# First mixer of a hybrid decoder: low parts of the weights made by accumulating loads, state scaling on VectorE

## The chip, the cores and the metric

The kernel runs on one core of a Trainium2 chip. A core has a matrix engine (TensorE, PE in the profile, with its weight loads as PEld), three engines for elementwise work (VectorE is DVE, ScalarE is ACT, GpSimd is POOL), and SyncE (SP), which here only issues transfers. The engines run their own instruction streams in order and wait for one another by semaphores. The metric is the device time of one execution in microseconds (us).

## The reference

One inference step of a small decoder: a Mamba-2 (SSD) mixer, a squared-ReLU MLP, an HGRN2 mixer and a second MLP, on 512 prompt tokens and 32 sample tokens (8 sequences of 4). Width is 1024. The change touches the SSD mixer alone; its core is

```python
proj = u @ w_in                                    # z, x/B/C, dt
xbc = silu(conv(xbc_ext) + conv_b)
def step(h, inp):                                  # chunks of 64 tokens
    ...
    y = einsum('bijgr,bjgrp->bigrp', cb * decay * dtq, xq)
    y = y + einsum('bign,bgrpn->bigrp', cq, h) * exp(cum)
    h = exp(cum[:, -1]) * h + einsum('bjgr,bjgrp,bjgn->bgrpn', tail, xq, bq)
    ...
y = group_rmsnorm((y + xs * d_skip) * silu(z), norm_w, 4)
return y @ w_out, new_conv, h
```

The line with `exp(cum[:, -1]) * h` is the state scaling that the change moves. The state is an output as well, for the prompt and for each sample sequence.

## The kernel before

All activations stay on chip, transposed: 1024 features as 8 tiles of 128 rows by 544 tokens (512 + 32). The products keep float32 accuracy by splitting both operands into a high part, which TensorE takes exactly, and the low rest, and by adding three products: high by high, high by low, low by high.

The weights of the whole network are streamed from memory as 224 units `W[u]` of 128x1024 float32 (512 KB): units 0 to 55 are the first mixer's (in and out projections interleaved), 56 to 119 the first MLP's (a Strassen form that also uses sums of blocks), 120 to 159 the second mixer's, 160 to 223 the second MLP's. A unit goes through these steps:

- `load_next` takes a buffer `raw` of the pool `wraw` (3 buffers) and issues the load on SyncE's queue (L170). In the MLPs it also forms sums `v` of two blocks, the second added by a load that accumulates, issued by GpSimd (L180).
- `conv_unit` calls `split` (L186 to L188): ScalarE casts `raw` to the high part `whi` (pool `wcv`, 2 buffers), then `wlo = raw - whi` is formed on VectorE. For units 4 to 55 whose number is divisible by 3 (17 of them) the subtraction is on GpSimd.
- `products` (L278 to L288) runs 48 matmuls for the unit.

`take` and `unit` keep the conversion one unit ahead of the products. A scheduler fixes the order of the instructions on each engine when the kernel is built, by program order and priority; `conv_unit` has high priority. Pools limit how far a step can run ahead: a tile can be written again only when the last reader of its buffer is done. PSUM has two accumulators of two banks (`acc`) and four of one bank (`mx`).

Beside the products of units 0 to 55 runs the rest of the mixer, as generators that are stepped while the products are issued: the convolution (L438 to L462: `pre`, `cacc`, `th`, `xs`), the step sizes (`dt_steps`, L771 on: `pcum`, `pdec`), and for each of 4 groups of heads `scan(g)` (L527) and `gated_norm` (L727). `scan` works on four chunks of 128 prompt tokens: `weights(c)` loads rows of the running sum (`w<-cum_d`) and takes the exponential on ScalarE, `tokens(c)` makes `xd` and `xt`, `inside(c)` computes the chunk's state contribution `pu` from `bt` and `xt`, scales the state `hT` in place (L569, GpSimd, chunks 1 to 3, so 12 times in all), adds `pu` (L570, VectorE) and adds the chunk's own output `py` to `y`; `before(c)` adds the earlier state's. Then the sample tokens: `xq` is split in two VectorE instructions (L685), the four state tiles `st` (two sequences each, 128x1024) are used in `psi`, scaled in place (L699, GpSimd, 16 in all), and 8 matmuls `pn` (L708) of `bm` and `xq` are added to them (L709, VectorE) before they are written out.

Of the kernel before, what the change touches and what calls it, by code (L numbers as in the profile page):

```python
# [10 lines left out]
F32R = mybir.dt.float32r  # L11
I32 = mybir.dt.int32
AF = mybir.ActivationFunctionType
ALU = mybir.AluOpType
ADD, SUB, MUL, MAX, MIN = ALU.add, ALU.subtract, ALU.mult, ALU.max, ALU.min

P = 128
# [31 lines left out]
U_MLP = U_SSD_OUT + 16  # L49
# [47 lines left out]
def trunk(ctx: ExitStack, tc: tile.TileContext, io):  # L97
    nc = tc.nc
# [1 line left out]

    const = ctx.enter_context(tc.tile_pool(name="const", bufs=1))
    pers = ctx.enter_context(tc.tile_pool(name="pers", bufs=1))
    wraw = ctx.enter_context(tc.tile_pool(name="wraw", bufs=3))
    wcv = ctx.enter_context(tc.tile_pool(name="wcv", bufs=2))
    psb = ctx.enter_context(tc.tile_pool(name="psb", bufs=2, space=PS))
    psm = ctx.enter_context(tc.tile_pool(name="psm", bufs=4, space=PS))
# [30 lines left out]
    loaded = {("u", i): t for i, t in enumerate(first)}  # L137
# [27 lines left out]
    def load_next():  # L165
        kind, u = loads[state["load"]]
        state["load"] += 1
        if kind == "u":
            raw = wraw.tile([P, 1024], F32, tag="raw", name=f"raw{u}")
            nc.sync.dma_start(raw, io["W"][u])  # L170
        elif kind == "a22":
            raw = mp["w"].tile([P, 512], F32, tag="a22", bufs=2, name=f"a22_{u}")
            nc.sync.dma_start(raw, io["W"][u + 1][:, 512:])
        else:

            raw = mp["w"].tile([P, 1024], F32, tag="v", bufs=3, name=f"v{u}")
            nc.sync.dma_start(raw[:, :512], io["W"][u + 1][:, 512:])
            nc.sync.dma_start(raw[:, 512:], io["W"][u][:, :512])
            for c in (0, 512):
                nc.gpsimd.dma_start(raw[:, c : c + 512], io["W"][u + 1][:, :512], accum_op=ADD)  # L180
        loaded[kind, u] = raw
# [4 lines left out]
    def split(raw, hi, lo, eng=None):  # L186
        nc.scalar.copy(hi, raw)  # L187
        (eng or nc.vector).tensor_tensor(lo, raw, hi.bitcast(F32), SUB)  # L188

    def conv_unit():  # L190
        if state["conv"] >= len(jobs):
            return
        (kind, u), at = jobs[state["conv"]]
        state["conv"] += 1
        with tc.high_priority() if u > 2 else ExitStack():
            while state["load"] <= min(at + (3 if mp else 1), len(loads) - 1):
                if loads[state["load"]][0] != "u" and not mp:
                    break
                load_next()
        with tc.high_priority() if u > 2 and not mp else ExitStack():  # L200
            if kind == "u":
                raw = loaded.pop(("u", u))
                hi = wcv.tile([P, 1024], F32R, tag="whi", name=f"whi{u}")
                lo = wcv.tile([P, 1024], F32R, tag="wlo", name=f"wlo{u}")
                for a in (0, 512) if u < 2 else (None,):
                    c = slice(None) if a is None else slice(a, a + 512)
                    split(raw[:, c], hi[:, c], lo[:, c], nc.gpsimd if 3 < u < U_MLP and u % 3 == 0 else None)
            else:
                hi, lo = form(kind, u)
        ready[kind, u] = (hi, lo)  # L210

    def form(name, u):

        a1 = loaded["u", u]
        v = loaded.get(("v", u))
        if name == "n6":
            s2 = mp["w"].tile([P, 512], F32, tag="s2", bufs=2, name=f"s2_{u}")
            nc.vector.tensor_tensor(s2, v[:, :512], a1[:, :512], ADD)
            loaded["s2", u] = s2
        if name == "q7":  # L220
            s2 = loaded["s2", u]
            nc.vector.tensor_tensor(s2, s2, a1[:, 512:], ADD)
        raw = {
            "p1": lambda: a1[:, :512], "p2": lambda: a1[:, 512:], "n6": lambda: s2, "q7": lambda: v[:, 512:],
            "n5": lambda: v[:, :512], "p3": lambda: loaded["s2", u], "q4": lambda: loaded["a22", u],
        }[name]()
        hi = mp["w"].tile([P, 512], F32R, tag="fh", bufs=5, name=f"fh{u}_{name}")
        lo = mp["w"].tile([P, 512], F32R, tag="fl", bufs=5, name=f"fl{u}_{name}")
        split(raw, hi, lo)
        return hi, lo  # L230

    def take(key):
        i = place[key]
        ahead = 0.0
        j = i
        while j + 1 < len(jobs) and ahead < 1.0:
            j += 1
            ahead += 1.0 if jobs[j][0][0] == "u" else 0.25
        while state["conv"] <= j:
            if jobs[state["conv"]][0][0] != "u" and not mp:  # L240
                break
            conv_unit()
        return ready.pop(key)
# [50 lines left out]
    def mx(name):  # L294
        return psm.tile([P, 512], F32, tag="mx", name=name)
# [82 lines left out]
    def ssd(then):  # L378
# [23 lines left out]


        conv_unit()
        conv_unit()
        xh = [pool.tile([P, 4, T], F32R, tag="y", bufs=2, name=f"xh{i}") for i in range(2)]
        xops = []
        for k in range(KT):
            lo = pool if k < 4 else p2
            lo = lo.tile([P, T], F32R, tag=f"yh{k}" if k < 4 else ("BT", "CT")[k % 2], name=f"xl{k}")  # L410
# [116 lines left out]
        def scan(g, BT, CT, xs, par):  # L527

            cum_d, dec, tok, ttok, etok = par
            pace = PACE[g]  # L530
            hs = slice(8 * g, 8 * g + 8)
# [28 lines left out]
            def inside(c):  # L560

                cs = slice(c * P, (c + 1) * P)
                pu = mx(f"pu{g}_{c}")
                nc.tensor.matmul(pu, bt[:, c], xts[c].rearrange("p h q -> p (h q)"), start=True, stop=True)
                if c == 0:
                    nc.scalar.copy(hT, pu)
                else:
                    hv = hT.rearrange("p (h q) -> p h q", q=64)
                    nc.gpsimd.tensor_tensor(hv, hv, dec[:, hs, c : c + 1].to_broadcast([P, 8, 64]), MUL)  # L569
                    nc.vector.tensor_tensor(hT, pu, hT, ADD)  # L570
                py = mx(f"py{g}_{c}")
                for h in range(8):
                    nc.tensor.matmul(
                        py[64 * (h % 2) : 64 * (h % 2) + 64, (h // 2) * P : (h // 2 + 1) * P], xds[c][:, h], ws_[c][:, h],
                        start=True, stop=True,
                    )
                nc.vector.tensor_tensor(y[:, :, cs], py.rearrange("p (j t) -> p j t", t=P), y[:, :, cs], ADD)
# [110 lines left out]
            for s in range(SEQS):  # L688
                c = s % 4
# [6 lines left out]
                ysc, psi.rearrange("p (h q) -> p h q", q=64), etok[:, hs].unsqueeze(2).to_broadcast([P, 8, 64]), MUL  # L696
            )
            for q in range(4):
                nc.gpsimd.tensor_tensor(  # L699
                    sts[q].rearrange("p s (h q) -> p s h q", q=64), sts[q].rearrange("p s (h q) -> p s h q", q=64),  # L700
                    dec[:, hs, 4 + 2 * q : 6 + 2 * q].rearrange("p h s -> p s h").unsqueeze(3).to_broadcast([P, 2, 8, 64]), MUL,
                )
# [815 lines left out]
```

## Time and profile before

| quantity | value |
|---|---|
| median of 3 runs | 1586.72 us (1585.82 to 1588.2) |
| the profiled execution | 1590.45 us |
| its span in the trace | 1588.7 us |
| mean granted TensorE clock | 0.985 |
| memory traffic | 164.00 MB read, 17.18 MB written |
| weight units on GpSimd (wlo, L188) | 17, mean 2.485 us |
| weight loads on SyncE (raw) | 198 of 512 KB, median 3.6 us to landing |

The profile gives, for one execution, the busy time of each engine, the TensorE clock that was granted, who waited for whom, and groups of like instructions. `out<-in` names the tile that an instruction writes and those it reads, with the buffer numbers left out; L188 is line 188 of the kernel. The lines themselves are shown where they are used.

### The profile page before, as it was taken

The page shows a single profiled execution, that of the slowest core. Times are in us where ns is not written, and L with a number is a line of the kernel's source. Part 1 is how long each engine was busy: PE and PEld are TensorE (multiplying, and loading weights), DVE is VectorE, ACT ScalarE, POOL GpSimd, SP SyncE. Part 2 cuts the span into 40 slices and gives each one's busy share as a digit, 9 for nine tenths or more (in the row PEclk, how much of TensorE's full clock was granted, in tenths as well). Part 3 has the DMA queues.
Part 4 walks back from the last instruction along what each step waited for, and adds up shares of the span by engine and source line. Part 5 has one row for each costly group of instructions (what it writes and reads, how often), then busy time and mean ns, then how long its engine had stood idle before and what let it go on. Part 6 is the DMA issues. An engine that isn't in the chain of part 4 may idle for free.

```text
span 1588.7 us, 32391 instructions
## 1 busy us (share of the span) xinstructions
PE 1547.5 (97%) x13420; PEld 1482.7 (93%) x13420; DVE 1099.3 (69%) x1962; ACT 741.9 (47%) x1431; POOL 187.9 (12%) x208
## 2 busy tenths in 40 slices
PE   8898989999999999999999999999999999999997
PEld 7896879999999999999999999999999999999997
DVE  7888787877887747464565688888878655474644
ACT  5585663757434526353463333333335436273552
POOL 4323141232311001010000000000001001010001
PEclk9998998999999999999999999999999999999998
DMA  5353435354236236344323232323226335453311
GB/s 185 104 164 105 159 88 187 102 176 143 74 120 175 91 107 172 94 136 104 112 64 126 67 96 83 98 83 116 77 94 173 88 106 153 120 160 80 120 54 57
DMA packets 88116, 183.28 MB, mean 115 GB/s; under 512 B 12641, under 2 KB 39297, under 8 KB 87969
## 3 DMA queue, kind: packets, MB, share of 16 engines
q1 hardware_dynamic: 79792, 167.49, 33.7%
q0 software_dynamic: 6912, 12.59, 4.9%
q8 instruction: 105, 1.72, 0.5%
q10 hardware_dynamic: 1264, 1.14, 0.2%
q14 instruction: 43, 0.34, 0.1%
HBM read 164.00 MB, written 17.18 MB: 114 GB/s over the span
## 4 chain that ended last, share of the span: by engine, by line
PE 71%; DVE 4%; ACT 1%; DMA 1%; issue 1%; POOL 0%; POOLq 0%; SPq 0%; ACTq 0%; DVEq 0%
PE pd L284 22%; PE ps L284 15%; PE pp L973 11%; PE pm L284 6%; PE pc L973 4%; PE pho L284 3%; PE po L284 2%; PE pa L1112 1%; DVE wlo L188 1%; ACT whi L187 1%; DMA raw<-in_W 1%; PE pS L1215 0%; PE po L1238 0%; PE pa L1131 0%; PE pd L1342 0%
## 5 line engine op out<-in xcount | busy, mean ns | idle before, releaser
L187 ACT CAST whi<-raw 128x1024 fp32r<-128x1024 f32 (+1 forms) x178 | 185.0, 1039 | 344.7 <-PE ps L284 110.7
L188 DVE TENSOR_TENSOR wlo<-raw,whi 128x1024 fp32r<-128x1024 f32 (+1 forms) x161 | 200.5, 1245 | 31.0 <-ACT whi L187 27.0
L284 PE MATMUL pd<-gh,wlo 128*128 128x272 f32 x992 | 205.5, 288 | 0.9 <-DVE wlo L188 0.6
L284 PE MATMUL pd<-gh,whi 128*128 128x272 f32 x992 | 205.7, 287 | 0.0
L284 PE MATMUL pd<-gl,whi 128*128 128x272 f32 x992 | 205.0, 288 | 0.0
L284 PEld LDWEIGHTS pd<-gh,wlo 128*128 128x128 f32 x992 | 155.7, 188 | 2.2 <-DVE wlo L188 2.2
L284 PEld LDWEIGHTS pd<-gh,whi 128*128 128x128 f32 x992 | 156.2, 188 | 0.0
L284 PEld LDWEIGHTS pd<-gl,whi 128*128 128x128 f32 x992 | 155.6, 188 | 0.0
L284 PE MATMUL ps<-uh_s,whi 128*128 128x272 f32 x576 | 127.4, 303 | 1.6 <-DVE zs L503 0.8
L373 DVE TENSOR_TENSOR x<-pd,x 128x544 f32<-128x544 f32 x62 | 44.7, 722 | 121.3 <-PE pd L284 121.3
L284 PE MATMUL ps<-ul_s,whi 128*128 128x272 f32 x576 | 122.5, 294 | 0.5 <-DVE ul_s L188 0.5
L284 PE MATMUL ps<-uh_s,wlo 128*128 128x272 f32 x576 | 121.7, 293 | 0.0
L180 POOL DMA_DIRECT2D v<-in_W x48 | 42.3, 1045 | 593.0 <-DMA v<-in_W 448.6
L284 PE MATMUL ps<-uh,whi 128*128 128x272 f32 x512 | 112.2, 300 | 0.0
L284 PE MATMUL ps<-uh,wlo 128*128 128x272 f32 x512 | 106.8, 288 | 0.0
L284 PE MATMUL ps<-ul,whi 128*128 128x272 f32 x512 | 106.4, 289 | 0.0
L284 PEld LDWEIGHTS ps<-uh_s,whi 128*128 128x128 f32 x576 | 93.0, 194 | 9.7 <-issue 5.6
L284 PEld LDWEIGHTS ps<-ul_s,whi 128*128 128x128 f32 x576 | 93.6, 195 | 1.0 <-DVE ul_s L188 0.7
L284 PEld LDWEIGHTS ps<-uh_s,wlo 128*128 128x128 f32 x576 | 92.7, 193 | 0.1
L284 PEld LDWEIGHTS ps<-uh,whi 128*128 128x128 f32 x512 | 80.6, 189 | 3.8 <-issue 1.4
L284 PEld LDWEIGHTS ps<-ul,whi 128*128 128x128 f32 x512 | 80.3, 189 | 0.0
L284 PEld LDWEIGHTS ps<-uh,wlo 128*128 128x128 f32 x512 | 80.2, 188 | 0.0
(428 smaller groups left out, 3894.1 us busy)
## 6 DMA issues: line engine op xcount, KB each, us to landing
raw<-in_W SPq DMA_DIRECT2D x198, 512.0 KB, 3.6
v<-in_W SPq DMA_DIRECT2D x48, 256.0 KB, 4.3
v<-in_W POOLq DMA_DIRECT2D x48, 256.0 KB, 5.8
st<-in_ssm_in SPq DMA_DIRECT2D x16, 512.0 KB, 5.7
w<-cum_d SPq DMA_DIRECT2D x16, 512.0 KB, 5.2
out_ssm_s<-st SPq DMA_DIRECT2D x16, 512.0 KB, 3.7
a<-in_W SPq DMA_DIRECT2D x24, 256.0 KB, 4.0
hst<-in_hgrn_in SPq DMA_DIRECT2D x8, 512.0 KB, 3.7
```

The costliest lines, as they stand in the source:

```text
L180: nc.gpsimd.dma_start(raw[:, c : c + 512], io["W"][u + 1][:, :512], accum_op=ADD)
L187: nc.scalar.copy(hi, raw)
L188: (eng or nc.vector).tensor_tensor(lo, raw, hi.bitcast(F32), SUB)
L284: nc.tensor.matmul(ps[:, h, :HF], w[:, k, :], o[:, h * HF : (h + 1) * HF], start=(first and k == 0 and j == 0), stop=(last and k == n - 1 ...
L373: nc.vector.tensor_tensor(v3(x[m]), ps[:, :, :HF], v3(x[m]), ADD)
L973: nc.tensor.matmul(ps, w[:, k, :], o, start=(name_ in ("p1", "p2", "q7") and k == 0 and j == 0), stop=(k == 3 and j == 2), skip_group_chec ...
L1112: nc.tensor.matmul(pv4[b * NS : (b + 1) * NS, c], K[:, bs], QQ[:, 2 - n :, bs], start=True, stop=True, tile_position=(0, b * NS),)
```

## The change

For units 4 to 55 the high part stays a cast on ScalarE, but no engine subtracts any more. As soon as a unit's high part is cast, `added_low` makes the next unit's low part: ScalarE writes `-raw` into `wlo`, whose type (float32r) cuts it to minus the high part, and GpSimd then issues a load of the same unit of `W` from memory that adds onto it, which leaves `W - hi`. `wlo` has 3 buffers in place of 2, and `wraw` 2 in place of 3 for the whole kernel. The scaling of `hT` and of the sample states goes from GpSimd to VectorE. Units 0 to 3, the MLPs and the second mixer keep `split`.

```diff
-    wraw = ctx.enter_context(tc.tile_pool(name="wraw", bufs=3))
+    wraw = ctx.enter_context(tc.tile_pool(name="wraw", bufs=2))
...
                 hi = wcv.tile([P, 1024], F32R, tag="whi", name=f"whi{u}")
-                lo = wcv.tile([P, 1024], F32R, tag="wlo", name=f"wlo{u}")
-                for a in (0, 512) if u < 2 else (None,):
-                    c = slice(None) if a is None else slice(a, a + 512)
-                    split(raw[:, c], hi[:, c], lo[:, c], nc.gpsimd if 3 < u < U_MLP and u % 3 == 0 else None)
+                if added(u):
+                    nc.scalar.copy(hi, raw)
+                else:
+                    lows[u] = wcv.tile([P, 1024], F32R, tag="wlo", bufs=3, name=f"wlo{u}")
+                    for a in (0, 512) if u < 2 else (None,):
+                        c = slice(None) if a is None else slice(a, a + 512)
+                        split(raw[:, c], hi[:, c], lows[u][:, c])
+                lo = lows.pop(u)
+                if added(u + 1):
+                    added_low(u + 1)
...
+    def added(u):
+        return 3 < u < U_MLP
+
+    def added_low(u):
+
+        while ("u", u) not in loaded:
+            load_next()
+        lows[u] = wcv.tile([P, 1024], F32R, tag="wlo", bufs=3, name=f"wlo{u}")
+        nc.scalar.activation(lows[u], loaded["u", u], AF.Copy, scale=-1.0)
+        nc.gpsimd.dma_start(lows[u], io["W"][u], accum_op=ADD)
...
-                    nc.gpsimd.tensor_tensor(hv, hv, dec[:, hs, c : c + 1].to_broadcast([P, 8, 64]), MUL)
+                    nc.vector.tensor_tensor(hv, hv, dec[:, hs, c : c + 1].to_broadcast([P, 8, 64]), MUL)
...
-                nc.gpsimd.tensor_tensor(
+                nc.vector.tensor_tensor(
                     sts[q].rearrange("p s (h q) -> p s h q", q=64), sts[q].rearrange("p s (h q) -> p s h q", q=64),
```

In the changed kernel lines from about L210 on stand 19 lower (L685 is L704 there). In the rows below a name carries the tile's own number and then a buffer number: `xq0` is group 0's, `wlo16` unit 16's.

VectorE, around the sample states of group 0, before:

```order
L570 TENSOR_TENSOR hT0_1056<-pu0_3_1624,hT0_1056 128x512
L448 SCALAR_TENSOR_TENSOR cacc7_1523<-pre7_1516,vh_129,cacc7_1523 128x568
L577 TENSOR_TENSOR y0_1132<-py0_3_1628,y0_1132 128x4x128
L188 TENSOR_TENSOR wlo16_1692<-raw16_1535,whi16_1691 128x1024
L448 SCALAR_TENSOR_TENSOR cacc7_1523<-pre7_1516,vh_129,cacc7_1523 128x568
L685 TENSOR_TENSOR xq0_1639<-xts0_1564,xq0_1639 32x512
L448 SCALAR_TENSOR_TENSOR cacc7_1523<-pre7_1516,vh_129,cacc7_1523 128x568
L685 TENSOR_TENSOR xq0_1639<-xts0_1564,xq0_1639 32x512
L695 TENSOR_TENSOR ysc0_1664<-psi0_1655,etok_869 128x512
L709 TENSOR_TENSOR st0_0_1057<-pn0_0_1720,st0_0_1057 128x512
```

The same place after (`L588` and `L718` are the moved scalings):

```order
L588 TENSOR_TENSOR hT0_1067<-hT0_1067,dec_871 128x512
L467 SCALAR_TENSOR_TENSOR cacc7_1537<-pre7_1530,vh_129,cacc7_1537 128x568
L589 TENSOR_TENSOR hT0_1067<-pu0_3_1639,hT0_1067 128x512
L467 SCALAR_TENSOR_TENSOR cacc7_1537<-pre7_1530,vh_129,cacc7_1537 128x568
L596 TENSOR_TENSOR y0_1143<-py0_3_1643,y0_1143 128x4x128
L467 SCALAR_TENSOR_TENSOR cacc7_1537<-pre7_1530,vh_129,cacc7_1537 128x568
L704 TENSOR_TENSOR xq0_1654<-xts0_1579,xq0_1654 32x512 x2
...
L714 TENSOR_TENSOR ysc0_1679<-psi0_1670,etok_877 128x512
L718 TENSOR_TENSOR st0_0_1068<-st0_0_1068,dec_871 128x1024
...
L718 TENSOR_TENSOR st0_3_1074<-st0_3_1074,dec_871 128x1024
L467 SCALAR_TENSOR_TENSOR cacc17_1692<-pre17_1685,vh_129,cacc17_1692 128x568
L728 TENSOR_TENSOR st0_0_1068<-pn0_0_1736,st0_0_1068 128x512
```

The subtraction of unit 16 is gone from the rows ahead of `xq0`, one scaling of `hT0` has come in, and the four scalings of the states stand behind `xq0` and `ysc0`, ahead of the first add of `pn`.

ScalarE, ahead of the copy `bt1` of group 1 (L617 before, L636 after), before:

```order
L187 CAST whi21_2163<-raw21_2018 128x1024
L187 CAST yh0_3_2072<-y0_1132 128x544
L556 ACTIVATE xt1_0_2104<-pxt1_0_2097,ttok_866 128x64 x8
...
L187 CAST whi22_2263<-raw22_2161 128x1024
L606 ACTIVATE y1_2152<-xs1_3_1407,vec_76 128x544
L482 ACTIVATE thz19_2157<-ps19_2024 128x544
L617 COPY bt1_2226<-pbt1_2216 128x512
```

And after:

```order
L560 ACTIVATE w1_1_2252<-w1_1_2252,tok_733 128x128 x4
L205 CAST whi20_2039<-raw20_1977 128x1024
L228 ACTIVATE wlo21_2041<-raw21_2037 128x1024
...
L205 CAST whi21_2183<-raw21_2037 128x1024
L228 ACTIVATE wlo22_2185<-raw22_2181 128x1024
...
L205 CAST whi22_2284<-raw22_2181 128x1024
L228 ACTIVATE wlo23_2286<-raw23_2282 128x1024
...
L501 ACTIVATE thz19_2177<-ps19_2044 128x544
L636 COPY bt1_2247<-pbt1_2237 128x512
```

Behind the first use of `w1_1` (L541 before, L560 after) three negations now stand ahead of `bt1`, each right behind the cast of the unit before.

GpSimd, over the same stretch as VectorE's rows, before:

```order
L188 TENSOR_TENSOR wlo15_1538<-raw15_1408,whi15_1537 128x1024
L462 COPY xs1_1_1167<-xs1_1_1167 128x96
L569 TENSOR_TENSOR hT0_1056<-hT0_1056,dec_863 128x512
L438 MEMSET pre17_1670 128x3
L442 COPY pre17_1670<-cst_127 128x8x3
L462 COPY xs1_2_1267<-xs1_2_1267 128x96
L699 TENSOR_TENSOR st0_0_1057<-st0_0_1057,dec_863 128x1024
```

After:

```order
L229 DMA wlo15_1425<-in_W 128x1024
L229 DMA wlo16_1553<-in_W 128x1024
L481 COPY xs1_1_1178<-xs1_1_1178 128x96
L457 MEMSET pre17_1685 128x3
L461 COPY pre17_1685<-cst_127 128x8x3
L481 COPY xs1_2_1279<-xs1_2_1279 128x96
L229 DMA wlo17_1708<-in_W 128x1024
```

GpSimd keeps its small copies and clears, and issues one accumulating load for each unit.

More of the change, by code (lines that the diff above doesn't have):

```diff
@@ L210, in conv_unit @@
         ready[kind, u] = (hi, lo)
+    lows = {}
+    def added(u):
[6 more added lines that the diff above has]
+        nc.gpsimd.dma_start(lows[u], io["W"][u], accum_op=ADD)
     def form(name, u):
```

## The prediction

> **What bounds the kernel now.** The page of the profile comes first: the busy row of TensorE (PE), its granted clock in 40 slices, and the chain that ended last.
>
> ```profile
> PE 1547.5 (97%) x13420; PEld 1482.7 (93%) x13420; DVE 1099.3 (69%) x1962; ACT 741.9 (47%) x1431; POOL 187.9 (12%) x208
> PEclk9998998999999999999999999999999999999998
> PE 71%; DVE 4%; ACT 1%; DMA 1%; issue 1%; POOL 0%; POOLq 0%; SPq 0%; ACTq 0%; DVEq 0%
> ```
>
> TensorE is the bound. Work taken off VectorE (DVE) or GpSimd (POOL) is worth only what TensorE idles for it, and the clock is below 9 tenths only early. So the next view is the busy time by windows (window, length, busy of PE, PEld, DVE, ACT and POOL with counts, granted clock, DMA share, GB/s).
>
> ```profile
> 40.00:80.00 40.00, 36.19 (x257) 33.85 (x258) 34.53 (x57) 19.68 (x42) 12.60 (x13) 0.91 0.36 106
> ...
> 120.00:160.00 40.00, 32.14 (x241) 27.81 (x240) 35.55 (x49) 21.05 (x51) 15.78 (x16) 0.87 0.36 116
> 160.00:200.00 40.00, 36.78 (x270) 35.35 (x269) 29.89 (x51) 25.74 (x58) 5.67 (x6) 0.91 0.47 146
> 200.00:240.00 40.00, 34.26 (x268) 28.79 (x268) 35.17 (x47) 24.80 (x69) 16.24 (x15) 0.92 0.35 89
> 240.00:280.00 40.00, 38.12 (x281) 37.38 (x280) 28.42 (x52) 16.49 (x32) 5.41 (x7) 0.91 0.56 192
> ...
> 500.00:600.00 100.00, 100.00 (x796) 99.59 (x795) 62.76 (x95) 40.33 (x62) 2.18 (x3) 1.00 0.40 109
> ```
>
> From 500 us on TensorE is full (796 matmuls in 100 us, 0.126 us each, so 6.0 us for the 48 of a weight unit). Five windows of the first mixer are not: they idle 3.8, 7.9, 3.2, 5.7 and 1.9 us, 22.5 in all. The waits, asked for about each hole, name the cause (engine, line, what it waited for; us, times, longest).
>
> ```profile
> PE pdec L819 <- DVE dt_md L809: 1.6, 1, 1.6
> PE pcum L814 <- DVE dt_tmp L807: 0.8, 1, 0.8
> ...
> PE pn L708 <- DVE xq L685: 7.9, 1, 7.9
> ...
> PE pu L564 <- ACT bt L617: 3.2, 1, 3.2
> ...
> PE pn L708 <- DVE xq L685: 5.7, 1, 5.7
> PE gn_pc L319 <- DVE ssq L345: 1.9, 1, 1.9
> ```
>
> I call them A (1.6 + 0.8, near 70 us), B (7.9, at 138), C (3.2, at 191), D (5.7, at 230) and E (1.9, at 259). Four wait for VectorE, C for ScalarE (ACT). Behind each hole the clock is halved for a while; the same window view, cut there, says so.
>
> ```profile
> 70.00:76.80 6.80, 5.43 (x21) 4.12 (x22) 3.46 (x7) 3.70 (x13) 1.56 (x4) 0.50 0.48 167
> 141.70:151.90 10.20, 5.54 (x21) 5.18 (x22) 8.95 (x13) 2.06 (x3) 3.36 (x5) 0.50 0.36 118
> 192.90:199.70 6.80, 5.75 (x20) 4.72 (x21) 6.37 (x8) 3.48 (x10) 0.19 (x2) 0.50 0.30 82
> 233.80:240.70 6.90, 4.92 (x18) 4.57 (x19) 6.82 (x8) 0.40 (x1) 3.63 (x2) 0.51 0.14 28
> 261.10:268.00 6.90, 6.90 (x32) 6.90 (x33) 3.52 (x14) 3.01 (x7) 0.00 (x0) 0.51 0.44 141
> ```
>
> Half of TensorE's busy time there is lost: 2.7, 2.8, 2.9, 2.5 and 3.4 us. With its idle time a hole costs A 5.1, B 10.7, C 6.1, D 8.2, E 5.3 us, together 35.4. That is nearly all that any change outside the matmuls can win.
>
> [...]
>
> **Why VectorE is late.** The timeline of VectorE ahead of B, and GpSimd's row over the same time (start, duration):
>
> ```profile
> 130.36 0.81 DVE L448 SCALAR_TENSOR_TENSOR cacc<-pre,vh,cacc 128x568 f32<-128x568 f32 x1
> ...
> 134.94 2.11 DVE L448 SCALAR_TENSOR_TENSOR cacc<-pre,vh,cacc 128x568 f32<-128x568 f32 x1
> ...
> 137.57 2.36 DVE L188 TENSOR_TENSOR wlo<-raw,whi 128x1024 fp32r<-128x1024 f32 x1
> 139.85 2.47 DVE L448 SCALAR_TENSOR_TENSOR cacc<-pre,vh,cacc 128x568 f32<-128x568 f32 x1
> 142.35 2.30 DVE L685 TENSOR_TENSOR xq<-xts,xq 32x512 fp32r<-32x512 f32 x1
> ...
> 145.53 0.69 DVE L685 TENSOR_TENSOR xq<-xts,xq 32x512 fp32r<-32x512 f32 x1
> ```
>
> ```profile
> 134.51 9.61 POOL L699 TENSOR_TENSOR st<-st,dec 128x1024 f32<-128x1024 f32 x4
> ```
>
> While GpSimd scales the four sample states, the same VectorE forms take 2.11 to 2.47 us instead of 0.81 and 0.69; from these rows the stretch is 1.3 + 1.1 + 1.7 + 1.6 = 5.7 us (the wlo at its usual 1.245, below). The two engines hold each other up; at B that is most of the wait.
>
> **The change, part by part.** Prices by group (count | busy us, mean ns):
>
> ```profile
> L188 POOL TENSOR_TENSOR wlo<-raw,whi 128x1024 fp32r<-128x1024 f32 x17 | 42.2, 2485 | 115.3 <-ACT whi L187 115.3
> L699 POOL TENSOR_TENSOR st<-st,dec 128x1024 f32<-128x1024 f32 x16 | 34.9, 2208 | 5.0 <-PE psi L690 5.0
> L569 POOL TENSOR_TENSOR hT<-hT,dec 128x512 f32<-128x512 f32 x12 | 15.3, 1273 | 36.2 <-PE pi L589 27.8 <-issue 8.4
> ```
>
> ```profile
> L188 DVE TENSOR_TENSOR wlo<-raw,whi 128x1024 fp32r<-128x1024 f32 (+1 forms) x161 | 200.5, 1245 | 31.0 <-ACT whi L187 27.0
> ...
> L598 DVE TENSOR_TENSOR w<-w,cb 128x1024 f32<-128x1024 f32 x16 | 19.4, 1221 | 6.0 <-ACT w L542 5.9
> ...
> L570 DVE TENSOR_TENSOR hT<-pu,hT 128x512 f32<-128x512 f32 x12 | 8.2, 681 | 3.4 <-PE pu L564 2.0 <-POOL hT L569 1.3
> ```
>
> *VectorE and GpSimd.* Of the 52 changed units 17 were subtracted on GpSimd, 35 on VectorE. VectorE loses 35 x 1.245 = 43.6 us and takes on 16 state scalings, priced by the equal form at L598 (1.221, 19.5 us), and 12 of hT, by L570 (0.681, 8.2 us): net 15.9 us less, and every stretch of the kind shown goes, since GpSimd keeps only short copies, clears and the issue of transfers. At B the subtraction of wlo16 (1.2) and the stretch (5.7) leave the row of xq, one hT scaling (0.7) enters it: xq is ready 6.2 us earlier, against 7.9. What VectorE is late by before 134 us, from the same cause, can give the rest. The state scalings come behind xq and ahead of the adds of pn, 4 x 1.22 = 4.9 us; four accumulators of PSUM take pn meanwhile, so nothing waits if TensorE has products to run. I take B, D, A and E as closed: **-29.3 us** (10.7 + 8.2 + 5.1 + 5.3). Ends: if a leftover of 1.7 us stays at B and one like it at D, each with its half-clock stretch (2.8 + 2.5), and A and E stay, the gain is only 18.9 - 1.7 x 2 - 5.3 = 10.2; the other end is all 35.4.
>
> *ScalarE.* A negation of 128x1024 for each of 52 units, beside the cast of the same size:
>
> ```profile
> L187 ACT CAST whi<-raw 128x1024 fp32r<-128x1024 f32 (+1 forms) x178 | 185.0, 1039 | 344.7 <-PE ps L284 110.7
> ...
> 176.71 0.69 ACT L541 ACTIVATE w<-w,tok 128x128 f32<-128x128 f32 x2 [6.71 <-DMA w<-cum_d]
> ```
>
> That is 52 x 1.039 = 54 us more work in 500 us; ScalarE is 16 to 26 busy of 40 in the windows above, so on average it has room. At C it has not: after 6.71 us of waiting for w (second row) it runs a backlog up to bt, on which TensorE waits. The order places three negations more between that wait and bt: 3 x 1.04 = 3.1 us. And the load of w stands on SyncE's queue behind a weight load that with two buffers waits for an earlier cast; from the times of casts I estimate 3.6 us. So C grows by 6.7, **+7 us**. Ends: 0, if other transfers are not held and the backlog is shorter, and 10. Elsewhere a negation that waits for its weight load holds what stands behind it on ScalarE, casts and PSUM copies: I take **+4 us** (ends 0 and the rival below).
>
> *The accumulating loads.* 52 transfers of 512 KB, issued by GpSimd. The trace has none of this size; near it stand plain loads, and accumulating loads of 256 KB (median us to landing in a window that holds one or two):
>
> ```profile
> raw<-in_W SPq DMA_DIRECT2D x198, 512.0 KB, 3.6
> ...
> raw<-in_W SPq DMA_DIRECT2D x1, 512.0 KB, 8.4
> ...
> v<-in_W POOLq DMA_DIRECT2D x1, 256.0 KB, 3.9
> ...
> v<-in_W POOLq DMA_DIRECT2D x2, 256.0 KB, 11.2
> ```
>
> Ends 3.9 (alone) and 11.2 (six queued at once, near 1202 us); I take 6, nearer the lone one, since here one follows another at 6 us or more. The time there is for it: with two hi buffers the cast of unit u+1 starts when TensorE starts u, the negation of u+2 ends 2.1 later, and u+2 starts at 12.0: 9.9 us. So at 6 nothing waits: **0**. At 11.2 each unit of the dense stretch (units 40 to 55, back to back) waits 1.3, +20.
>
> *Two raw buffers.* In the MLPs and the second mixer a weight load now starts one unit (6.0 us) later.
>
> ```profile
> SPq L170 <- DVE wlo L188: 645.4, 122, 25.4
> ```
>
> The SyncE queue waited for a free buffer at 122 loads already, so loads were early; at 3.6 us landing one unit is still ahead. I take **+1.5** (ends 0 and 3; the short Strassen weights at a group's start are the tight places).
>
> Sum: -29.3 + 7 + 4 + 0 + 1.5 = -16.8. From the profiled execution's 1590.45 us (1588.7 of span and 1.75 around it) that gives 1573.7. The median of the runs shown is 1586.72, 3.7 lower, so the forecast in their terms is **1570 us**.
>
> **The rivals.** *1, slower: ScalarE is held by raw loads.* Place: the negation right behind each cast, in order on ScalarE, waiting for a weight load that started only a unit ago. It decides where that load lands later than a unit takes. For it: DMA share is 0.35 to 0.56 already, 52 x 512 KB come on top, and one load here took 8.4. Against: the median is 3.6. If loads land at 11 us, 26 of the 52 units (the closer half, spaced near 6) are held 5 us each, 130 us; half of that reaches TensorE, +65. With -29.3, +7 and +1.5 that is +44: 1631 by the medians. Loads near 8.4 (2.4 x 26 / 2 = 31, net +10, 1597) are about where it turns. *2, all holes close* and nothing new opens: -35.4, **1551**; for it speaks that VectorE gets 16 us back and C's wait may shift with it. *3, holes trade places:* the gain of B and D is eaten by accumulating loads at 11.2 (+20 - 16.8): 1590, or by holes as large elsewhere: about **1587**. *4, the change does nothing it says:* the order of instructions shows the transfers and negations, so this has no chance worth naming.
>
> [...]
>
> **How the numbers follow.** Forecast (1560 to 1580) 0.45; rival 2 (1545 to 1560) 0.18; rival 3 (1580 to 1594) 0.2; rival 1 (1594 to 1631) 0.17. 0.2% is 3.2 us, about what a measurement of this kernel can tell. Faster takes the forecast, rival 2 and half of rival 3 (0.73), the same a third of rival 3 and a little of rival 1 (0.09), slower the rest (0.18). The range leaves out the far part of rival 1 and a little below: 1547 to 1598.
>
> **What would show it.** Right: no xq waits by pn of more than 2 us, VectorE rows at L467 (was 448) and L704 (was 685) near 0.8 and 0.7, clock 1.00 in the windows 120 to 160 and 200 to 240, a larger hole at bt near 190 us, accumulating loads landing near 6 us. Wrong: TensorE waiting for wlo or whi in units 4 to 55 (rivals 1, 3), ScalarE idle before the negation for a DMA (rival 1), holes in the MLPs behind a raw load, or new half-clock stretches at other lines.

## The result, and the profile after

The changed kernel takes 1598.83 us (median of 4 runs, 1598.1 to 1604.89) beside 1586.27 for the kernel before: a ratio of 1.0086, 95% interval 1.0059 to 1.0112. It is slower by about 13 us; the forecast was 1570 and faster. The profiled execution took 1598.18 us. That of before (1590.45) lay 3.7 us over the median of 1586.72, so the two traces differ by 7.7 us only. Executions of one kernel spread by some us, and the traces of e5, e6, e11 and e13 below are each of the fastest one, 5 to 8 us under its median.

The page of the changed kernel, the same three rows as before:

```profile
PE 1550.5 (97%) x13420; PEld 1485.0 (93%) x13420; DVE 1038.5 (65%) x1955; ACT 785.1 (49%) x1483; POOL 136.7 (9%) x215
...
PEclk9999898999999999999999999999999999999998
...
PE 70%; ACT 2%; DVE 2%; issue 1%; DMA 1%; POOL 0%; POOLq 0%; SPq 0%; ACTq 0%
```

VectorE is relieved (1099 to 1039 us), ScalarE has more (742 to 785), TensorE is the bound as before. In the chain VectorE went from 4% to 2%, and ScalarE from 1% to 2%. The windows of the first mixer (busy of PE, PEld, DVE, ACT, POOL, clock, DMA share, GB/s):

```profile
120.00:160.00 40.00, 37.36 (x302) 33.31 (x301) 37.23 (x66) 29.87 (x65) 7.29 (x16) 1.00 0.75 187
160.00:200.00 40.00, 30.30 (x197) 28.89 (x198) 19.62 (x37) 25.91 (x58) 3.45 (x4) 0.81 0.79 201
200.00:240.00 40.00, 39.81 (x321) 34.54 (x320) 30.89 (x50) 27.52 (x71) 4.47 (x12) 0.98 0.59 129
240.00:280.00 40.00, 36.38 (x258) 34.93 (x256) 22.55 (x49) 18.99 (x34) 5.36 (x10) 0.87 0.90 240
```

The windows of B and D (120 to 160, 200 to 240) are nearly full now, with clocks of 1.00 and 0.98 instead of 0.87 and 0.92. The time is lost at 160 to 200 and 240 to 280, where the clock is 0.81 and 0.87, and the share of the transfer engines, which was 0.35 to 0.56 in these four windows, is 0.59 to 0.90. (The share adds up the times of all packets, and can pass 1: it is 1.06 between 260 and 280 us. It measures load, and is no filling level.) The waits of TensorE around its holes:

```profile
PE pn L727 <- DVE xq L704: 1.3, 1, 1.3
...
PE ps L303 <- DVE zs L502: 3.9, 1, 3.9
...
PE pu L583 <- ACT bt L636: 6.2, 1, 6.2
...
PE po L303 <- ACT pre L460: 3.6, 1, 3.6
...
PE po L303 <- ACT pre L460: 2.3, 1, 2.3
```

B has shrunk from 7.9 to 1.3 and A, D and E are gone. C has doubled, from 3.2 to 6.2. New are one of 3.9 at 159 us, two (at 243 and 281) where TensorE waits for ScalarE to copy `pre` out of PSUM, and smaller ones (2.0 us at 45, 1.0 to 1.5 at 97, 345, 381 and 408). All of TensorE's waits between 36 and 520 us add up to 27.4 us, beside 24.4 before. The half-clock stretches of the first mixer add up to 34.1 us, beside 37.6 before: there are five, as there were, at other places. At one of the new holes the timeline of ScalarE shows what stands ahead of the copy (start, duration, in brackets the idle time before it and who ended it):

```profile
243.43 0.63 ACT L605 ACTIVATE E<-E 128x512 f32<-128x512 f32 x1 [5.67 <-DMA E<-cum_d]
243.96 1.03 ACT L205 CAST whi<-raw 128x1024 fp32r<-128x1024 f32 x1
244.90 1.05 ACT L228 ACTIVATE wlo<-raw 128x1024 fp32r<-128x1024 f32 x1
245.86 0.36 ACT L458 COPY pre<-ps 128x272 f32<-128x272 f32 x1
```

ScalarE stood idle for 5.67 us until the load of `E` had landed, with the cast, the negation and the three copies of `pre` (the first is shown) in order behind it. The transfers between 40 and 480 us say why (KB each, median us to landing; for the queues MB and the share of 16 engines). Before:

```profile
q1 hardware_dynamic: 40095, 56.37, 42.7%
...
raw<-in_W SPq DMA_DIRECT2D x50, 512.0 KB, 3.6
st<-in_ssm_in SPq DMA_DIRECT2D x16, 512.0 KB, 5.7
w<-cum_d SPq DMA_DIRECT2D x16, 512.0 KB, 5.2
...
E<-cum_d SPq DMA_DIRECT2D x24, 128.0 KB, 4.2
```

And in the changed kernel:

```profile
q1 hardware_dynamic: 40008, 56.02, 42.1%
q0 software_dynamic: 7054, 25.69, 34.6%
...
raw<-in_W SPq DMA_DIRECT2D x50, 512.0 KB, 3.6
wlo<-in_W POOLq DMA_DIRECT2D x49, 512.0 KB, 7.0
st<-in_ssm_in SPq DMA_DIRECT2D x16, 512.0 KB, 9.0
w<-cum_d SPq DMA_DIRECT2D x16, 512.0 KB, 6.2
...
E<-cum_d SPq DMA_DIRECT2D x24, 128.0 KB, 7.2
```

The added loads land in 7.0 us, in time for their units: no wait of TensorE for `wlo` in this trace comes from a load. But the state loads went from 5.7 to 9.0 and E from 4.2 to 7.2, and ScalarE's waits grew with them. Before, between 36 and 500 us:

```profile
ACT w L541 <- DMA w<-cum_d: 15.4, 7, 6.7
...
ACT E L586 <- DMA E<-cum_d: 7.4, 4, 3.9
```

After:

```profile
ACT w L560 <- DMA w<-cum_d: 21.9, 8, 11.6
ACT E L605 <- DMA E<-cum_d: 18.8, 6, 5.7
```

Theory S, formed from this: the added loads fill the 16 transfer engines, other loads come late, and ScalarE, in order, passes that on. Its rivals: the negations alone make ScalarE late (N); the weight loads that wait for one of two buffers hold the loads of w and E behind them on SyncE's queue (Q).

### The profile page after: what moved, and what is told of

Same layout as the page of the kernel before. It is cut to its first block, busy times and chain, and to the rows that moved or that the text cites. A ratio compares the mean times of both kernels' runs of the same rounds, so it can differ in the third digit from the quotient of the medians.

```text
span 1596.4 us, 32412 instructions
## 1 busy us (share of the span) xinstructions
PE 1550.5 (97%) x13420; PEld 1485.0 (93%) x13420; DVE 1038.5 (65%) x1955; ACT 785.1 (49%) x1483; POOL 136.7 (9%) x215
## 4 chain that ended last, share of the span: by engine, by line
PE 70%; ACT 2%; DVE 2%; issue 1%; DMA 1%; POOL 0%; POOLq 0%; SPq 0%; ACTq 0%
PE pd L303 22%; PE ps L303 14%; PE pp L992 11%; PE pm L303 6%; PE pc L992 4%; PE pho L303 3%; PE po L303 3%; PE pa L1131 1%; PE po L1257 0%; PE pS L1234 0%; PE pa L1150 0%; DVE wlo L188 0%; PE pd L1361 0%; DMA raw<-in_W 0%; ACT whi L187 0%
## 5 line engine op out<-in xcount | busy, mean ns | idle before, releaser
L187 ACT CAST whi<-raw 128x1024 fp32r<-128x1024 f32 (+1 forms) x126 | 130.5, 1035 | 305.9 <-PE pd L303 132.6
L188 DVE TENSOR_TENSOR wlo<-raw,whi 128x1024 fp32r<-128x1024 f32 (+1 forms) x126 | 153.1, 1215 | 14.2 <-ACT whi L187 9.8
```

## The experiments

Medians in us, and ratios to the kernel before on the same chips with their 95% intervals:

| run | what it is | median | ratio |
|---|---|---|---|
| e3 | changed, added load of 64 columns | 1572.5 | 0.9927 (0.9908 to 0.9946) |
| e5 | changed, 512 columns | 1576.9 | 0.9936 (0.9919 to 0.9953) |
| e16 | changed, 768 columns | 1584.6 | 0.9991 (0.9980 to 1.0002) |
| e6 | changed, 1024 columns without adding | 1578.6 | 0.9953 (0.9937 to 0.9968) |
| e13 | changed, w and E loads small | 1584.7 | 0.9991 (0.9973 to 1.0008) |
| e7 | changed, w and E loads from ScalarE | 1628.1 | 1.0262 (1.0242 to 1.0283) |
| e4 | changed, 3 raw and 2 wlo buffers | 1655.7 | 1.0444 (1.0419 to 1.0470) |
| e11 | changed, negations on VectorE | 1598.1 | 1.0062 (1.0043 to 1.0081) |
| e10 | changed, scalings back on GpSimd | 1608.5 | 1.0128 (1.0110 to 1.0146) |
| e2 | before, scalings on VectorE | 1591.7 | 1.0034 (1.0022 to 1.0046) |
| e9 | before, all subtractions on VectorE | 1584.6 | 0.9976 (0.9967 to 0.9985) |
| e1 | before, both of these | 1572.1 | 0.9912 (0.9897 to 0.9926) |
| e8 | before, 2 raw buffers | 1590.0 | 1.0019 (1.0010 to 1.0029) |
| e14 | e1 with 2 raw buffers | 1576.5 | 0.9931 (0.9919 to 0.9943) |
| e15 | e14 with 3 whi buffers | 1577.7 | 0.9942 (0.9929 to 0.9955) |
| e12 | changed, 17 added loads only | 1574.1 | 0.9913 (0.9898 to 0.9928) |

### The traffic of the added loads: e3, e5, e6, e16

```diff
-        nc.gpsimd.dma_start(lows[u], io["W"][u], accum_op=ADD)
+        nc.gpsimd.dma_start(lows[u][:, :64], io["W"][u][:, :64], accum_op=ADD)
```

> The changed kernel with the accumulating load cut to the first 64 of 1024 columns (the low parts of units 4 to 55 are then minus the high part in the other columns: the addition of W is left out there). All instructions, negations, waits and the order stay; 25 MB of traffic goes. Theory S (loads of w and E come late because the transfers share engines, and ScalarE stands): w and E land in 5 and 4 us again, ScalarE's waits for them fall from 41 to some 23 us, and the time falls to 1578 to 1588. Theory N (the negations themselves make ScalarE late): the time stays at 1594 to 1600.

With every instruction, buffer and wait left in place and only the bytes gone, the kernel takes 1572.5: 26.3 us less. That is the largest effect of the study, and beyond the band that either theory gave. Its transfers:

```profile
q1 hardware_dynamic: 41446, 59.58, 44.9%
q0 software_dynamic: 7586, 2.37, 5.3%
...
st<-in_ssm_in SPq DMA_DIRECT2D x16, 512.0 KB, 6.3
w<-cum_d SPq DMA_DIRECT2D x16, 512.0 KB, 5.5
...
E<-cum_d SPq DMA_DIRECT2D x24, 128.0 KB, 4.0
```

```profile
ACT w L560 <- DMA w<-cum_d: 9.8, 5, 6.1
ACT E L605 <- DMA E<-cum_d: 4.4, 4, 3.1
```

State, w and E are back near their times of before, and ScalarE's waits for w and E fall from 40.7 to 14.2 us (9.8 + 4.4). TensorE's waits between 36 and 520 us fall from 27.4 to 9.7 us, and its half-clock stretches in the first mixer from 34.1 to 13.6. The holes at `pre` are gone but for 0.2 us, C is back at 3.3, and only the 3.9 us for `zs` stands as it was, so the added bytes do not make that one. Of the 28.1 us between the two traces 27.4 lie in the first mixer: the first MLP's first matmul starts at 495.9 us in the changed kernel and at 468.5 in e3.

Theory N falls: the 52 negations are all there. Theory Q, taken alone, falls as well: e3 has the same two buffers, and SyncE's queue waits for casts there nearly as long (48 times, 243.3 us, beside 253.8). One more rival is that the traffic slows the engines' own instructions. The rows exclude it: the convolution on VectorE (L467) takes 0.802 us in the changed kernel and 0.803 in e3, the negation 1.062 and 1.069. Next come half the columns, and the whole load without adding:

```diff
-        nc.gpsimd.dma_start(lows[u], io["W"][u], accum_op=ADD)
+        nc.gpsimd.dma_start(lows[u][:, :512], io["W"][u][:, :512], accum_op=ADD)    # e5
...
+        nc.gpsimd.dma_start(lows[u], io["W"][u])                                     # e6
```

> The changed kernel with the added load cut to 512 of 1024 columns (the addition of W to the other half is left out). The full load measured 1598.8 us and 64 columns 1572.5. Theory S (shared transfer engines, dose by bytes): about in the middle, 1582 to 1589. If there is a threshold (a transfer only hurts once it fills the engines beside a state load), it stays near the low end, 1572 to 1578.

> The changed kernel with the second load of each unit written plainly over wlo, without adding (the low parts are then W itself; the subtraction is left out). Same bytes from memory, same queue, same waits. In the trace of the changed kernel the accumulating queue moved 39.85 MB in 15.2% of the engines' time and the other queue 167.49 MB in 33.8%, so an added byte takes 1.9 times as long. Theory R (the adding itself is what fills the engines): 1582 to 1589, as with half the bytes. Theory B (bytes count, added or not): 1595 to 1601.

Half the columns cost 4.4 us of the 26.3 by the medians, and 1.4 by the ratios, whose intervals overlap; either is far from half, so the cost is not linear in bytes. The same 512 KB written plainly cost 6.1 by the medians and 4.1 by the ratios, less than theory R had and far from theory B. The queue's row of e6 (between 40 and 480 us):

```profile
q0 software_dynamic: 7385, 26.56, 20.4%
```

Without adding, 26.56 MB take 20.4% of the engines in 440 us, 3.4 us of all sixteen for a MB; with adding, 25.69 MB take 34.6%, 5.9 us. A byte that was added cost the engines 1.75 times a byte that was written. So bytes do not tell what a load costs here; the engines' busy share (second number from the end) does, in one window for each kernel. Changed:

```profile
40.00:480.00 440.00, 412.82 (x3196) 383.16 (x3197) 297.09 (x525) 297.35 (x643) 60.50 (x116) 0.96 0.77 187
```

With 64 columns (e3):

```profile
40.00:480.00 440.00, 431.06 (x3416) 403.12 (x3417) 317.42 (x561) 308.80 (x660) 64.83 (x121) 0.98 0.51 142
```

With 512 (e5):

```profile
40.00:480.00 440.00, 428.08 (x3406) 399.82 (x3407) 316.50 (x561) 308.16 (x659) 63.27 (x121) 0.99 0.65 168
```

Without adding (e6):

```profile
40.00:480.00 440.00, 427.50 (x3383) 399.62 (x3383) 315.15 (x558) 309.70 (x660) 47.15 (x120) 0.98 0.65 197
```

e6 moves more GB/s than the changed kernel (197 to 187), and is 20 us faster. Half the columns and the plain load have the same share, 0.65, and within their intervals the same time. From 0.51 to 0.65 the cost is 1 to 6 us, from 0.65 to 0.77 it is 20 to 24 (by ratios and by medians). e16 tests this reading at a share that it predicts:

```diff
+        nc.gpsimd.dma_start(lows[u][:, :768], io["W"][u][:, :768], accum_op=ADD)
```

> The changed kernel with the added load cut to 768 of 1024 columns (the addition of W to the last 256 is left out); the loads of w and E stay whole. Between 40 and 480 us the transfer engines were busy 0.51 with 64 columns (1572.5 us), 0.65 with 512 (1576.9), 0.70 with whole loads but small w and E (1584.7) and 0.77 in the changed kernel (1598.8). If the engines' busy share decides, whichever transfers make it, this kernel has about 0.71 and comes to 1583 to 1589, like the run with small w and E. If w and E are special, it stays above 1591.

It measured 1584.6 at a share of

```profile
40.00:480.00 440.00, 420.84 (x3304) 391.58 (x3305) 308.44 (x542) 303.80 (x653) 59.88 (x116) 0.98 0.71 176
```

0.71, as expected. Theory S holds, with a knee between 0.65 and 0.77 among these five kernels, which differ in the added load alone. Where other things differ too, the share gives no time: e7 and e10, below, have 0.71 and 0.75, and are slower than the changed kernel.

### Over which transfers it goes: e13, e7, e4, e11

```diff
-                nc.sync.dma_start(w, cum_d[hs, c * P : (c + 1) * P].partition_broadcast(P))
+                nc.sync.dma_start(w[:, 7:8], cum_d[8 * g : 8 * g + 1, c * P : (c + 1) * P].partition_broadcast(P))
...
-                    nc.scalar.activation(w[:, h], w[:, h], AF.Relu, ...
+                    nc.scalar.activation(w[:, h], w[:, 7], AF.Relu, ...
...
+                    nc.sync.dma_start(E[64 * o : 64 * o + 64, 3:4], src[o][:1].partition_broadcast(64))
+                nc.scalar.activation(E[:, :3], E[:, 3:4].to_broadcast([P, 3, P]), AF.Exp)
+                nc.scalar.activation(E[:, 3:4], E[:, 3:4], AF.Exp)
```

> The changed kernel, its added loads whole, with each load of w cut to one of its 8 heads and each of E to one of 4 blocks, ScalarE reading that one for all (values of other heads are left out; instructions stay, one small one more for each E). Traffic falls by 11 MB, less than the 13 MB of the half load. If the added loads cost time because w and E land late, ScalarE's waits for them (41 us) fall under 15 and the time to 1575 to 1585. If the loss runs over weight and state loads instead, 1590 to 1600.

By the sizes of the loads the cut takes away 9.7 MB, not 11. 1584.7: 14 us less, at the upper edge of the first band, but ScalarE's waits for w stayed (22.9 us; for E 8.6, together 31.5 and not under 15). Its share is 0.70, and e16, with w and E whole at 0.71, has the same median. So the lower share is enough to explain this gain; that w and E are a way of their own is not shown.

```diff
-                nc.sync.dma_start(w, cum_d[...
+                nc.scalar.dma_start(w, cum_d[...
...
-                    nc.sync.dma_start(E[64 * o ...
+                    nc.scalar.dma_start(E[64 * o ...
```

> The changed kernel with the loads of w and E issued by ScalarE instead of SyncE, so that no weight load that waits for its buffer stands ahead of them. Theory Q (they are late because SyncE's queue is held): they go out earlier, ScalarE's waits for them (41 us now) fall below 20, 1580 to 1590. Theory S (they are late because the engines are shared): their time to landing stays at 6 to 7 us and the time at 1594 to 1602, or more, as ScalarE issues 64 transfers on top.

29 us worse than the changed kernel. From issue to landing w and E (40 transfers in all, not 64) took 5.9 and 4.6 us, less than in the changed kernel (6.2 and 7.2), and yet ScalarE's waits for w doubled to 43.2 us. So it is the issue that comes late: it now stands in ScalarE's own order. The new place was worse than the queue, and this run alone does not settle theory Q. For the same end

```diff
-    wraw = ctx.enter_context(tc.tile_pool(name="wraw", bufs=2))
+    wraw = ctx.enter_context(tc.tile_pool(name="wraw", bufs=3))
...
-                    lows[u] = wcv.tile([P, 1024], F32R, tag="wlo", bufs=3, name=f"wlo{u}")
+                    lows[u] = wcv.tile([P, 1024], F32R, tag="wlo", bufs=2, name=f"wlo{u}")
...
-        lows[u] = wcv.tile([P, 1024], F32R, tag="wlo", bufs=3, name=f"wlo{u}")
+        lows[u] = wcv.tile([P, 1024], F32R, tag="wlo", bufs=2, name=f"wlo{u}")
```

> The changed kernel with three raw buffers again and two wlo buffers. Theory Q (a weight load that waits for its buffer holds the loads of w and E behind it on SyncE's queue): weight loads no longer wait, w and E are issued earlier, 1580 to 1590. If the sharing of the transfer engines or the negations make the loss, it stays at 1595 to 1602; the two wlo buffers may add waits of the negation for the products of two units before.

1655.7, above every band. Its waits:

```profile
PE po L303 <- DMA wlo<-in_W: 25.1, 10, 4.3
PE ps L303 <- DMA wlo<-in_W: 22.9, 14, 3.2
```

With two `wlo` buffers the negation of u+1 waits for the products of u-1, the added load has one unit (6.0 us) to land and took 7.5, and TensorE waits for it 24 times, 48 us. The third `wlo` buffer is what keeps these waits away; as both changes are in it, the run says nothing on Q.

```diff
-        nc.scalar.activation(lows[u], loaded["u", u], AF.Copy, scale=-1.0)
+        nc.vector.tensor_scalar(lows[u], loaded["u", u], -1.0, None, MUL)
```

> The changed kernel with the 52 negations on VectorE; ScalarE loses 54 us of work, the traffic stays. If the late loads of w and E cost time only because ScalarE is full behind them, 1576 to 1588. If their lateness alone makes the holes, 1594 to 1605.

1598.1 (ratio 1.0062; its interval overlaps that of the change, whose ratio is 1.0086): taking 52 negations off ScalarE buys little or nothing while the traffic is there, as the second theory had it. VectorE has them instead, so a small gain may be hidden in it.

### GpSimd's part: e2, e9, e1, e10

```diff
-                    nc.gpsimd.tensor_tensor(hv, hv, dec...          # e2, e1
+                    nc.vector.tensor_tensor(hv, hv, dec...
...
-                nc.gpsimd.tensor_tensor(sts[q]...                   # e2, e1
+                nc.vector.tensor_tensor(sts[q]...
...
-                    split(raw[:, c], hi[:, c], lo[:, c], nc.gpsimd if 3 < u < U_MLP and u % 3 == 0 else None)   # e9, e1
+                    split(raw[:, c], hi[:, c], lo[:, c])
```

> The kernel before, with both scalings on VectorE and all 52 subtractions on VectorE, so GpSimd computes nothing large; no added loads, three raw buffers. VectorE gets 17 x 1.245 + 19.5 + 8.2 = 49 us more of its own work and loses the stretch. If it is the stretch beside GpSimd (and not VectorE's amount of work) that opens the holes at 138 and 230 us, these close and the time falls to about 1560 to 1570. If VectorE's amount of work decides, the time stays or rises: 1586 to 1600.

> The kernel before, with only the two scalings moved to VectorE (17 subtractions stay on GpSimd). The state scaling is what runs beside xq in the trace of before. Stretch theory: xq comes some 5 us earlier at 138 and 230, half to all of those holes goes, 1568 to 1578. Rival (VectorE's order and load): four scalings ahead of the adds of pn hold the copies behind, no gain, 1584 to 1594.

> The kernel before with the 17 GpSimd subtractions on VectorE and nothing else; the state and hT scalings stay on GpSimd. Both moved gave 1572.1, the scalings alone 1591.7, so moving the scalings in this company is worth what this kernel lies above 1572. If the state scalings beside xq make the holes at 138 and 230 us (the prediction's reading), those holes stay and the time is 1585 to 1598. If the subtractions on GpSimd were the harm, 1565 to 1575.

The scalings alone lose 0.34%, the subtractions alone win 0.24%, both win 0.88%: far from a sum. e1 comes out 2 us above its first band, e2 in the rival's, e9 half a us under its first. In e9, where the scalings are on GpSimd still, B and D stand as the prediction read them:

```profile
PE pn L708 <- DVE xq L685: 7.4, 1, 7.4
...
PE pn L708 <- DVE xq L685: 5.8, 1, 5.8
```

In e2, with the scalings away, they fall to

```profile
PE pn L708 <- DVE xq L685: 2.8, 1, 2.8
PE ps L284 <- DVE zs L483: 7.3, 1, 7.3
...
PE pn L708 <- DVE xq L685: 1.3, 1, 1.3
```

2.8 and 1.3, as the stretch theory had it, but the 7.3 us between them, for the gate `zs` at 162 us, is new against the kernel before (e9 waits 3.5 us there). In e1 D is 0.8, A is down to 0.3, C to 1.4, and the hole for `zs` stays:

```profile
PE ps L284 <- DVE zs L483: 8.2, 1, 8.2
```

So the gain of both moves is real (13.4 us by the medians) and needs both. VectorE's own extra work of 49 us did not keep the four holes from closing. Why the scalings alone lose time is not shown.

```diff
-                    nc.vector.tensor_tensor(hv, hv, dec...
+                    nc.gpsimd.tensor_tensor(hv, hv, dec...
...
-                nc.vector.tensor_tensor(sts[q]...
+                nc.gpsimd.tensor_tensor(sts[q]...
```

> The changed kernel with both scalings back on GpSimd: the added loads alone. If the holes at 138 and 230 come from the scalings, they return: 1605 to 1620. If the late transfers hide them, 1596 to 1602. If the scalings hurt on VectorE here too, as alone, under 1595.

1608.5: in the changed kernel too the scalings on VectorE are worth 7 us by the ratios and 10 by the medians, and the added loads with the two raw buffers, but without the scalings' move, cost 1.28%. B is back with 7.9 us.

### The buffers, and fewer added loads: e8, e14, e15, e12

```diff
-    wraw = ctx.enter_context(tc.tile_pool(name="wraw", bufs=3))
+    wraw = ctx.enter_context(tc.tile_pool(name="wraw", bufs=2))
```

> The kernel before with two raw buffers instead of three and nothing else: the price of that part alone. The prediction's term is 0 to 3 us in the later stages, so 1586 to 1590; if the first mixer pays too (loads of w and E held behind weight loads on SyncE's queue) 1592 to 1605.

> The kernel of all large elementwise work on VectorE (1572.1) with two raw buffers in place of three: the price of that part in a kernel whose holes are closed. Prediction's term: 0 to 3 us, so 1572 to 1575. If two buffers hold the loads of w and E behind them, 1578 or more.

Two raw buffers cost 0.19% in the kernel before and as much in e1 (0.9912 to 0.9931), some 3 us; by the medians of e14 and e1 it is 4.4, and their intervals overlap. The traces of e1 and e14 show where: up to the first matmul of the first MLP they take 473.8 and 474.0 us, from there to the last matmul 1088.3 and 1091.8. So the later stages pay 3.5 us and the first mixer 0.2. The later stages take 1088.9 us in the trace of before and 1090.5 in that of the changed kernel, 1.6 more.

```diff
+                hi = wcv.tile([P, 1024], F32R, tag="whi", bufs=3, name=f"whi{u}")
```

> The same kernel with two raw buffers and three for whi. It still has a hole of 8.2 us at 153 us, where ScalarE stands at a cast that waits for its whi buffer while VectorE waits for what is behind it. If the third whi buffer lets that cast go, the hole closes: 1560 to 1568. If the hole has another cause, 1571 to 1576.

No gain over e14, and a hole of 8.1 us stays near 154 us: it does not come from the `whi` buffers. The cause stays open.

```diff
-        return 3 < u < U_MLP
+        return 3 < u < U_MLP and u % 3 == 0
```

> The changed kernel with added loads for the 17 units divisible by 3 only, the other 35 subtracted on VectorE. Traffic is a third: by the dose seen (64 columns 1572.5, half 1576.9, full 1598.8) the traffic costs 1 to 4 us, and VectorE has 21 us less than with all 52 on it (1572.1): 1568 to 1577. If any added load beside a w or E load opens a hole of its own, 1578 to 1588.

1574.1 at a share of 0.58: a third of the added loads costs nothing that shows, and wins nothing over e1, though VectorE has 21 us less to do. e1 and e12 are the fastest of the kernels that compute all of the outputs; e1 is the simpler.

## Why the prediction was wrong, point by point

- **TensorE is the bound, the holes of the first mixer with their half clock are what there is to win.** Right: of the 28.1 us between the traces of e3 and the changed kernel, 27.4 lie in the first mixer, and TensorE's waits (17.7 us less) and its half-clock stretches (20.5 us shorter, some 8 us of lost matmul time) make up nearly all of it.
- **The state scalings on GpSimd stretch VectorE ahead of xq.** Right. In the trace of after the rows ahead of xq are short again:

```profile
137.17 0.79 DVE L467 SCALAR_TENSOR_TENSOR cacc<-pre,vh,cacc 128x568 f32<-128x568 f32 x1
138.00 1.38 DVE L704 TENSOR_TENSOR xq<-xts,xq 32x512 fp32r<-32x512 f32 x2
```

  0.79 instead of 2.1 to 2.5, 0.69 for each half of xq. A, D and E are gone and 1.3 us of B are left, inside the 1.7 that was the bad end.
- **-29.3 for the four holes.** They close, but the gain is about half as large. In e1, without added loads and with all subtractions on VectorE, A, B, D and E are gone or under 1 us, and the kernel wins 13.4 us: the hole of 8.2 us for `zs`, with 13.7 us at half clock behind it, takes their place. The changed kernel and e3 have 3.9 us there. The sum let nothing new open; rival 3 (holes trade places) named this, with a chance of 0.2.
- **Prices on the engines.** Right: the state scalings took 1.218 us on VectorE (1.221 forecast), the negations 1.062 on ScalarE (1.039).

```profile
L718 DVE TENSOR_TENSOR st<-st,dec 128x1024 f32<-128x1024 f32 x16 | 18.6, 1218 | 0.1
```

```profile
L228 ACT ACTIVATE wlo<-raw 128x1024 fp32r<-128x1024 f32 x52 | 55.2, 1062 | 7.5 <-DMA raw<-in_W 7.2 <-PE po L303 0.3
```

- **+7 at C, for three negations and a load held on SyncE's queue.** C grew by 3.0, and in e3, with the same negations and the same buffers, it is 3.3 us, as before. So it is the traffic, not the two causes given.
- **"So at 6 nothing waits: 0", the accumulating loads.** This is the step that failed. The deadline was right (landing 7.0 of 9.9 us, no wait for `wlo`), but the term asked only when the added load itself lands, and gave no price to what it does to the loads of others. That price is 26.3 us by the medians of e3 and the changed kernel (25 by their ratios), more than the whole forecast gain of 16.8. The runs show this in place of the 0: the added loads raise the share of the transfer engines from 0.51 to 0.77, E lands in 7.2 us and not 4.0, ScalarE waits 40.7 us for w and E and not 14.2, and TensorE waits for what stands behind them on ScalarE. Without the bytes the kernel measures 1572.5, 2.5 from the 1570 (11.6 us below before by the ratio, 13.8 by the medians, 20.4 by the spans of the traces, for 16.8 forecast). That it comes so near is in part luck: the hole for `zs` lowers the gain, and the +7 and +4 that were to lower it did not come.
- **Rival 1, slower by late loads.** Loads from SyncE's queue did land later beside the added loads from GpSimd's: E in 7.2 us, and in 4.0 with 64 columns, the state loads in 9.0 and 6.3. Rival 1 named the added traffic, but put the harm on the weight loads and on the negations that wait for them. Those still land in 3.6 us, and the negations waited 7.2 us in all; the state loads and those of w and E were the late ones, so its price (from 1597) and its chance of 0.17 were taken from a mechanism that did not run, and that 1598.8 lies in its band is chance. The DMA share that stood in the rows (0.35 to 0.56) was used as an argument, and never carried forward: 49 of the added loads fall between 40 and 480 us, where before the share is 0.43; at SyncE's price of 3.3 us for a MB they give 0.62, and at 1.75 times that price 0.77, which was measured.
- **+4 for negations elsewhere.** No sign of it: e3 has all of them, and beside C TensorE waits there for ScalarE only 1.1 us at `uh_s` and 0.2 at `pre` (0.8 and 0.4 before). No run prices the negations alone, without the traffic.
- **+1.5 for two raw buffers.** Right in place: the later stages paid 1.6 us in the changed kernel, and 3.5 in e14; e8 and e14 cost some 3 us in all.
- Not followed: the changed kernel takes 10.0 us from the start of its last matmul to the end, 2.1 more than before; the same stands in e3, not in e12.

## What to carry to other kernels

Before work is moved from an engine to a transfer, add up the transfer engines' busy share of that stage, with an accumulating load at its own measured price (here 1.75 times that of a plain one), and not the new load's own deadline alone; in these kernels the cost over the one with 64 columns (0.51) was 4 to 6 us by the medians at a share of 0.65, 12 at 0.71 and 26 at 0.77. What hurts by being late need not be the new load: here it was other loads, for which ScalarE, working in order, waited 40.7 us and not 14.2. And where two engines hold each other up (VectorE's rows at B took 2.1 to 2.5 us beside GpSimd's scalings, and 0.7 to 0.8 without), try the whole parting and not only a part of it: here one half of the move alone lost 0.34%, the other won 0.24%, and both together won 0.88%.

## What the runs showed of the hardware

- Between 40 and 480 us an accumulating load took the sixteen transfer engines 5.9 us for a MB (34.6% of 440 us for 25.69 MB, changed kernel), a plain load from the same queue 3.4 (20.4% for 26.56 MB, e6), one from SyncE's queue 3.3 (42.1% for 56.02 MB, changed kernel).
- Some short holes of TensorE counted twice in these traces, as idle time and as half clock behind them. The holes of 2.0 us at 44.6 and of 2.3 at 280.7 in the changed kernel were each followed by 3.4 us at half clock, that of 3.9 by 6.9, those of 3.6 and 6.2 by 10.2 us; those of 1.0 to 1.5 us (96.8, 345, 380.6, 408) by none. In the trace of before E, 1.9 us, was followed by 6.9 us at 0.51. The length of the hole does not settle it: C, with 3.2 to 3.3 us, was followed by 6.8 us at half clock in the trace of before, by 3.4 in those of e3 and e6, and by none in those of e5 and e13.

```profile
48.20:51.60 3.40, 3.40 (x17) 3.40 (x17) 2.44 (x4) 2.93 (x4) 0.00 (x0) 0.50 0.31 60
...
191.60:201.80 10.20, 6.07 (x21) 5.04 (x22) 5.06 (x8) 6.81 (x12) 1.39 (x4) 0.50 0.57 116
...
283.70:287.10 3.40, 3.40 (x18) 3.40 (x17) 2.31 (x4) 3.12 (x10) 0.00 (x0) 0.50 0.96 187
```
